# Which PSUM banks the five two-bank products of the second feed-forward matmul take

## The chip, the cores and the metric

The kernel runs on one core of a Trainium2 chip. The metric is device microseconds (us) of one execution, lower is better. One execution was also taken by the hardware profiler, and every row below is from it.

## The reference

A two-layer transformer block on 512 tokens of width 1024 in float32. Each layer is a mixer (convolution, pooling, gating and sparse attention) and a feed-forward half; only the latter matters here:

```python
for l in range(2):
    ...
    h = rms_norm(x, pre_ffn_norm[l])
    f = jnp.square(jax.nn.relu(jnp.einsum('bsd,df->bsf', h, ffn_w1[l])))   # 512x1024 @ 1024x4096
    x = x + rms_norm(jnp.einsum('bsf,fd->bsd', f, ffn_w2[l]), post_ffn_norm[l])  # 512x4096 @ 4096x1024
```

## The kernel before, in words

**Precision.** Every float32 operand is split into a high and a low part, `wh` and `wl` for weights (`split`: one ScalarE activation for the high part, one VectorE subtraction for the low one). `mm3` replaces one product by three matmuls (high by high, high by low, low by high).

**The feed-forward half.** `ffn` cuts the 4096 hidden columns into four parts. In parts 0, 1 and 2 both matmuls are done by a seven-product scheme (Strassen-like) on 2 by 2 blocks. `square4` makes the hidden values of half a part: its products A11, A12, S1, S2, S3, S4, A22 run as 128x256 matmuls into `pf` banks, and VectorE and ScalarE turn them into the forms `A11` to `S4` that the second matmul reads (a form's high half by ScalarE, its low half by VectorE). The second matmul's seven products are p1, p7, p2, p5, p6, p3 and q4, in this order, as 128x512 matmuls, 24 for each product: two token halves by two weight units by six. p1 and p7 keep banks of their own for all three parts (`po`). The other five ask `banks()` for two PSUM banks (`pm`), one for each half, and `add_up` adds each half to a sum in SBUF when it is done: ScalarE copies in part 0, VectorE additions (`acc<-pm,acc`, or `y<-pm,y` for p2 and q4) in parts 1 and 2. Part 3 is done in the ordinary way.

**PSUM.** Eight banks in four groups: `mm` three, `o` one, `s` two (p7's here), `x` two (p1's here). `square4`'s `pf` tiles also use `mm` and `o`. A bank is free for the next tile when its last reader is done.

**Weights.** `load` brings 512 KB units from HBM on SyncE's queue into six raw buffers `wr`. Some products want a sum of weight blocks: `more` adds a further block to a raw buffer by an accumulating DMA on GpSimd's queue (POOL). p5's two units get one each, p7's two get one and then, after they were split, another for p6 and another for q4. An accumulate into a buffer waits until the load, or the split, before it is done.

**What sets the order.** `_Rec` records all operations, and `order()` then writes the order of every engine by list scheduling: it has a cost for each operation, a delay for each pair of engines, and the number of buffers of each pool, and takes at each step the operation that can start first by these. So a change of a bank's group can move instructions on every engine, and whatever is late on the chip is waited for in that fixed order, since each engine works its list from front to back. All instructions show as line 442 (`issue`).

Of the kernel before, what the change touches and what calls it, by code (L numbers as in the profile page):

```python
# [19 lines left out]
P = 128  # L20
# [424 lines left out]
SUMS, CONV, POST, FORM, FORM2, FORM3, C11 = 300, -300, -1000, -1000, 0, 500, 500  # L445


TAGS = "mm", "o"
FIN = (1, 1), (1, 0)


class _Net:
# [907 lines left out]
    def ffn(self, l, norm):  # L1360


        (_, (F, _)), y = norm
        ssv = self.small.tile([P, NT, 2], F32, name=self.nm("ssv"), tag="ssv", bufs=2)
        accs = [y, self.big("acc", F32), self.big("acc", F32)]
        acc = {"q4": accs[0][:, 0:2], "p2": accs[0][:, 2:4], "p5": accs[1][:, 0:2], "p6": accs[1][:, 2:4],
               "p3": accs[2][:, 0:2]}

        own = {"p1": [self.pst([P, 512], "po", "x") for _ in range(2)],
               "p7": [self.pst([P, 512], "po", "s") for _ in range(2)]}  # L1370

        u0 = U_FF
        for part in range(NPART - 1):
            uw = u0 + PART
            form, raw = {}, {}

            def put(name, bh, v):
                if name not in form:
                    form[name] = self.big(name)
                o = slice(2 * bh, 2 * bh + 2)  # L1380
                hi = form[name][:, o, :256]
                self.act(hi, v)
                self.tt(form[name][:, o, 256:], v, hi.bitcast(F32), ALU.subtract)

            def emit0(bh, th, v):
                raw["A21" if th else "A11", bh] = v
                if not th:
                    put("A11", bh, v)
                if ("A11", bh) in raw and ("A21", bh) in raw:
                    s3 = self.scr("s3").rearrange("p (b q) -> p b q", b=2)  # L1390
                    self.tt(s3, raw["A11", bh], raw["A21", bh], ALU.subtract)
                    put("S3", bh, s3)

            def emit1(bh, th, v):
                raw["A22" if th else "A12", bh] = v
                if not th:
                    put("A12", bh, v)
                if ("A12", bh) in raw and ("A22", bh) in raw:
                    a11, a21, a12, a22 = (raw[n, bh] for n in ("A11", "A21", "A12", "A22"))
                    self.tt(a21, a22, a21, ALU.subtract)  # L1400
                    put("S1", bh, a21)
                    self.stt(a11, a21, -1.0, a11, ALU.mult, ALU.subtract)
                    put("S2", bh, a11)
                    self.stt(a12, a11, -1.0, a12, ALU.mult, ALU.subtract)
                    put("S4", bh, a12)
                    put("A22", bh, a22)

            def banks():
                return [self.pst([P, 512], "pm", TAGS[i]) for i in range(2)]

            def product(pss, units, a, first=True, final=True):

                for u in range(2):
                    wh, wl = units(u)
                    for t in range(2):
                        c = slice(P * t, P * t + P)
                        d = slice(256 + P * t, 256 + P * t + P)
                        for kk in range(2):
                            k = 2 * u + kk
                            o = slice(512 * kk, 512 * kk + 512)  # L1420
                            self.mm3(pss[t], a[:, k, c], a[:, k, d], wh[:, o], wl[:, o], first and k == 0,
                                     final and k == 3)

            def add_up(name, pss):
                for i in range(2):
                    v = acc[name][:, i]
                    if part == 0:
                        self.act(v, pss[i])
                    else:
                        self.tt(v, pss[i], v, ALU.add)  # L1430

            more = lambda x, i: self.nc.gpsimd.dma_start(x, self.a["wst"][l, i], accum_op=ALU.add)
            sq = [self.square4(l, u0 + 4 * i, F, e, y[:, i] if part == 0 else None)
                  for i, e in enumerate((emit0, emit1))]
            if part == 0:
                for _ in range(2):
                    for v in sq:
                        next(v)
            for _ in sq[0]:
                pass  # L1440

            raws = {}
            simple = lambda i: lambda j: self.split(self.load(l, uw + i + j))

            def weights(first, j, *steps):

                if (first, j) not in raws:
                    raws[first, j] = self.load(l, uw + first + j)
                x = raws[first, j]
                for i in steps:  # L1450
                    more(x, uw + i + j)
                return self.split(x)


            steps = {"p1": simple(0), "p2": simple(2), "p3": simple(6), "p5": lambda j: weights(0, j, 4),
                     "p7": lambda j: weights(4, j, 6), "p6": lambda j: weights(4, j, 0),
                     "q4": lambda j: weights(4, j, 2)}
            left = {"p1": "A11", "p7": "S3", "p2": "A12", "p5": "S1", "p6": "S2", "p3": "S4", "q4": "A22"}
            for name in ["p1", "", "p7", "p2", "p5", "p6", "p3", "q4"]:
                if not name:  # L1460
                    for _ in sq[1]:
                        pass
                elif name in own:

                    product(own[name], steps[name], form[left[name]], part == 0, part == NPART - 2)
                else:
                    ps = banks()
                    product(ps, steps[name], form[left[name]])
                    add_up(name, ps)
            u0 += 2 * PART  # L1470

        plus = lambda v, w: self.tt(v, w, v, ALU.add)
        f = [[self.big("f") for _ in range(2)] for _ in range(2)]

        def emit(i):
            def put(bh, th, v):
                o = slice(None), slice(2 * bh, 2 * bh + 2), slice(256 * th, 256 * th + 256)
                self.act(f[0][i][o], v)
                self.tt(f[1][i][o], v, f[0][i][o].bitcast(F32), ALU.subtract)
            return put  # L1480


        ys = {}
        self.nc.shift = SUMS
        for i in range(2):
            y11, y12, y21, U, w = (acc[n][:, i] for n in ("p2", "p3", "q4", "p6", "p5"))
            plus(U, own["p1"][i])
            plus(y11, own["p1"][i])
            plus(w, U)
            plus(y21, U)  # L1490
            plus(y12, w)
            plus(w, own["p7"][i])
            plus(y21, own["p7"][i])
            ys[i, 0], ys[i, 1], ys[2 + i, 0], ys[2 + i, 1] = y11, y12, y21, w
        self.nc.shift = 0
        for i in range(2):
            for _ in self.square4(l, u0 + 4 * i, F, emit(i)):
                pass
        srcs = [(f[0][k // 4][:, k % 4], f[1][k // 4][:, k % 4]) for k in range(PART)]
        g2, g0 = self.gains(*[(l, 3072), (l + 1, 0)][:1 + (l + 1 < L)])  # L1500
        uw = u0 + PART
        for t, ps in self.tgroup(lambda j: self.unit(l, uw + j), srcs, 2):
            v = ys[t, 0]
            plus(v, ps)
            self.square(v, ssv[:, t, 0:1])
            self.tt(v, v, g2[:, 0:512], ALU.mult)
        after = (g0, self.new_hT()) if l + 1 < L else None
        for t, ps in self.tgroup(lambda j: self.unit(l, uw + 4 + j), srcs, 4, own["p1"] + own["p7"]):
            v = ys[t, 1]
            self.nc.shift = POST  # L1510
            self.tt(v, ps, v, ALU.subtract)
            self.square(v, ssv[:, t, 1:2])
            self.nc.shift = 0
            self.tt(v, v, g2[:, 512:], ALU.mult)
            self.post(t, [ys[t, 0], v], ssv[:, t])
            if after:
                self.norm_tile(t, *after)
        return after
# [82 lines left out]
```

## Time and profile before

| | us |
|---|---|
| median of 3 runs | 1053.36 (1053.11, 1053.36, 1060.53) |
| profiled execution | 1053.45 |
| its span in the trace | 1051.7 |
| TensorE busy in the span | 1024.9 |
| VectorE busy | 824.8 |
| ScalarE busy | 611.0 |

PE is TensorE, DVE VectorE, ACT ScalarE, POOL GpSimd, SP SyncE. The ends of matmuls are modelled: a 128x512 matmul is shown with 0.39 us or more though the next one starts 0.23 us after it, so PE's busy time holds more than its pitch, and a wait costs a little more than the idle time that is shown. A group of rows such as `x2` stands for instructions in a row of one form. `[0.78 <-DVE acc]` says that the engine sat idle for 0.78 us before, and that a VectorE instruction writing `acc` ended it.

### The profile page before, as it was taken

The numbers are of one execution on the slowest core, as the hardware profiler recorded it, in microseconds if no ns is written. First come the engines' busy times: TensorE is split into PE (matmuls) and PEld (weight loads), VectorE is DVE, ScalarE is ACT, GpSimd is POOL, SyncE is SP. The second block draws the span as 40 slices with busy tenths as digits, with TensorE's granted clock in tenths as the row PEclk, the third lists the DMA queues.
The fourth block names the chain that finished last, engine by engine and source line by source line (L and its number), as shares of the span: only waits on it lengthen the run. The fifth ranks groups of instructions, "written<-read, shape, count | busy, mean of one in ns | idle before, by whom it ended". The sixth has DMA issues, their size and how long they took to land.

```text
span 1051.7 us, 17150 instructions
## 1 busy us (share of the span) xinstructions
PE 1024.9 (97%) x6706; PEld 891.7 (85%) x6706; DVE 824.8 (78%) x1250; ACT 611.0 (58%) x1057; POOL 137.6 (13%) x192
## 2 busy tenths in 40 slices
PE   7999999999999999999999999999999999999997
PEld 6998777898897898798899986779989978978985
DVE  7799976899478678976679998769985686798754
ACT  6437874676567366365444587658675655654731
POOL 3000011211121111110110000102211211211001
PEclk9999999999999999999999999999999999999999
DMA  8330244379989899986034110534998989989802
GB/s 296 115 122 21 61 124 115 73 186 232 227 217 229 222 245 216 215 248 215 22 95 138 60 56 26 120 101 98 223 224 212 235 207 235 243 189 245 232 4 80
DMA packets 47906, 168.89 MB, mean 161 GB/s; under 512 B 5713, under 2 KB 6609, under 8 KB 47570
## 3 DMA queue, kind: packets, MB, share of 16 engines
q0 software_dynamic: 16128, 58.73, 31.5%
q1 hardware_dynamic: 31698, 109.08, 30.2%
q8 instruction: 52, 0.85, 0.3%
q14 instruction: 28, 0.23, 0.1%
HBM read 165.69 MB, written 2.10 MB: 160 GB/s over the span
## 4 chain that ended last, share of the span: by engine, by line
PE 74%; DVE 11%; DMA 7%; issue 5%; ACT 3%; POOL 1%; POOLq 0%; DVEq 0%; SPq 0%; ACTq 0%
PE pf L442 24%; PE pm L442 22%; PE po L442 8%; PE pp L442 6%; DMA wr<-wst 6%; PE pc L442 3%; PE O L442 2%; PE s L442 2%; DVE wl L442 2%; PE ppt L442 2%; DVE cacc L442 2%; ACT wh L442 1%; PE pt L442 1%; POOL r L442 1%; PE ph L442 1%
## 5 line engine op out<-in xcount | busy, mean ns | idle before, releaser
L442 DVE TENSOR_TENSOR wl<-wr,wh 128x1024 fp32r<-128x1024 f32 (+1 forms) x256 | 305.0, 1205 | 95.1 <-ACT wh L442 93.8
L442 ACT ACTIVATE wh<-wr 128x1024 fp32r<-128x1024 f32 (+1 forms) x258 | 264.0, 1042 | 143.0 <-DMA wr<-wst 55.5
L442 PE MATMUL pf<-hF,wh 128*128 128x256 f32 x1728 | 300.8, 278 | 1.4 <-ACT wh L442 1.2
L442 PEld LDWEIGHTS pf<-hF,wh 128*128 128x128 f32 x1728 | 262.7, 188 | 6.3 <-ACT wh L442 2.2
L442 PE MATMUL pf<-hF,wl 128*128 128x256 f32 x864 | 239.0, 277 | 0.0
L442 POOL DMA_DIRECT2D wr<-wst x112 | 97.0, 900 | 511.6 <-DVE wl L442 255.2
L442 PEld LDWEIGHTS pf<-hF,wl 128*128 128x128 f32 x864 | 162.3, 188 | 0.8 <-DVE wl L442 0.2
L442 PE MATMUL pm<-wh,S 128*128 128x512 f32 x288 | 95.1, 400 | 6.5 <-DVE acc L442 4.1
L442 PE MATMUL pp<-wh,hT 128*128 128x256 f32 (+1 forms) x512 | 100.3, 287 | 0.0
L442 DVE SCALAR_TENSOR_TENSOR cacc<-rest,cwh,cacc 128x512 f32<-128x512 f32 x120 | 85.9, 742 | 0.4
L442 PE MATMUL pm<-wh,mixT 128*128 128x512 f32 x256 | 84.0, 401 | 1.2 <-DVE y L442 1.2
L442 PEld LDWEIGHTS pp<-wh,hT 128*128 128x128 f32 x512 | 80.6, 188 | 0.5
L442 PEld LDWEIGHTS pm<-wh,S 128*128 128x128 f32 x288 | 53.8, 188 | 25.3 <-DVE acc L442 6.7
L442 PE MATMUL pp<-wl,hT 128*128 128x256 f32 (+1 forms) x256 | 74.0, 289 | 0.0
L442 PE MATMUL pm<-wh,A 128*128 128x512 f32 x192 | 63.0, 395 | 0.0
L442 PE MATMUL pm<-wl,S 128*128 128x512 f32 x144 | 56.7, 396 | 3.3 <-DVE wl L442 3.3
L442 PEld LDWEIGHTS pm<-wh,mixT 128*128 128x128 f32 x256 | 47.8, 188 | 13.2 <-DVE y L442 2.0
L442 ACT ACTIVATE c<-c 128x512 f32<-128x512 f32 x64 | 37.8, 622 | 24.7 <-DVE c L442 24.4
L442 PE MATMUL pm<-wl,mixT 128*128 128x512 f32 x128 | 50.6, 395 | 0.0
L442 PEld LDWEIGHTS pp<-wl,hT 128*128 128x128 f32 x256 | 48.2, 188 | 0.3
L442 PE MATMUL pc<-hT,wh 128*128 128x256 f32 x256 | 47.4, 287 | 0.8 <-ACT hT L442 0.8
L442 POOL TENSOR_TENSOR r<-rs,mhalf 128x1 f32<-128x1 f32 x32 | 24.0, 750 | 158.2 <-DVE rs L442 158.2
(283 smaller groups left out, 1841.1 us busy)
## 6 DMA issues: line engine op xcount, KB each, us to landing
wr<-wst SPq DMA_DIRECT2D x182, 512.0 KB, 5.6
wr<-wst POOLq DMA_DIRECT2D x112, 512.0 KB, 7.1
gb<-rows SPq DMA_DIRECT2D x7, 512.0 KB, 5.9
wr<-wq SPq DMA_DIRECT2D x8, 268.0 KB, 2.8
xres<-x SPq DMA_DIRECT2D x4, 512.0 KB, 6.0
cw<-cw SPq DMA_DIRECT2D x2, 1024.0 KB, 7.2
out<-xres SPq DMA_DIRECT2D x3, 512.0 KB, 2.6
sgw<-sgw SPq DMA_DIRECT2D x2, 256.0 KB, 5.2
```

The costliest lines, as they stand in the source:

```text
L442: getattr(getattr(nc, e), method)(*[real(x) for x in args], **{k: real(x) for k, x in kw.items()})
```

## The change

`banks` gets the place `n` of the product in the list. A product at an odd place takes one `mm` bank and the `o` bank, one at an even place two `mm` banks. So p2 (3), p6 (5) and q4 (7) keep what they had, and p5 (4) and p3 (6) take two `mm` banks in place of one `mm` and the `o` bank. No operation is added or taken away; the order that `order()` writes differs on PE, ACT, DVE and POOL, and SP's is the same.

```diff
-TAGS = "mm", "o"
...
-            def banks():
-                return [self.pst([P, 512], "pm", TAGS[i]) for i in range(2)]
+            def banks(n):
+                return [self.pst([P, 512], "pm", "o" if i and n % 2 else "mm") for i in range(2)]
...
-            for name in ["p1", "", "p7", "p2", "p5", "p6", "p3", "q4"]:
+            for n, name in enumerate(["p1", "", "p7", "p2", "p5", "p6", "p3", "q4"]):
...
-                    ps = banks()
+                    ps = banks(n)
```

In the orders below a name carries the tile's number and then a number of its place, which differs between the two kernels; what counts is the first. `x2` is two in a row.

**PE where p5 begins, part 1 of layer 0.** `pm_579` and `pm_580` are p5's two halves, `pm_587` is p6's first half, `pm_593` p3's. Before:

```order
L442 MATMUL pm_572_3766<-wh_577_3676,A12_551_3624 128x512
L442 MATMUL pm_579_3800<-wh_582_3779,S1_559_3710 128x512
L442 MATMUL pm_587_3804<-wh_589_3759,S2_560_3719 128x512
L442 MATMUL pm_587_3804<-wl_590_3773,S2_560_3719 128x512
L442 MATMUL pm_587_3804<-wh_589_3759,S2_560_3719 128x512 x2
L442 MATMUL pm_587_3804<-wl_590_3773,S2_560_3719 128x512
L442 MATMUL pm_587_3804<-wh_589_3759,S2_560_3719 128x512
L442 MATMUL pm_587_3804<-wh_591_3787,S2_560_3719 128x512
L442 MATMUL pm_593_3820<-wh_596_3813,S4_561_3755 128x512
L442 MATMUL pm_580_3825<-wh_582_3779,S1_559_3710 128x512
L442 MATMUL pm_579_3800<-wl_583_3823,S1_559_3710 128x512
```

After:

```order
L442 MATMUL pm_572_3769<-wh_577_3678,A12_551_3624 128x512
L442 MATMUL pm_579_3801<-wh_582_3749,S1_559_3708 128x512
L442 MATMUL pm_579_3801<-wl_583_3761,S1_559_3708 128x512
L442 MATMUL pm_580_3807<-wh_582_3749,S1_559_3708 128x512
L442 MATMUL pm_580_3807<-wl_583_3761,S1_559_3708 128x512
L442 MATMUL pm_579_3801<-wh_582_3749,S1_559_3708 128x512 x2
L442 MATMUL pm_579_3801<-wl_583_3761,S1_559_3708 128x512
L442 MATMUL pm_579_3801<-wh_582_3749,S1_559_3708 128x512
L442 MATMUL pm_580_3807<-wh_582_3749,S1_559_3708 128x512 x2
L442 MATMUL pm_580_3807<-wl_583_3761,S1_559_3708 128x512
L442 MATMUL pm_580_3807<-wh_582_3749,S1_559_3708 128x512
L442 MATMUL pm_587_3827<-wh_589_3766,S2_560_3719 128x512
```

Both halves of p5's first unit now run ahead of p6, whose first half before came between p5's first matmul and the rest; p5's low part `wl_583` is wanted by the second matmul, not after ten of others.

**DVE at the same place.** `wl_583` is p5's first low part, `wl_592` p6's second, `s1_538` the end of `square4`'s last sum, `y_298` the sum of p2. Before, from the sum on:

```order
L442 TENSOR_TENSOR s1_502_3233<-s1_538_3524,s1_502_3233 128x512
L442 TENSOR_TENSOR wl_590_3773<-wr_565_3357,wh_589_3759 128x1024
...
L442 TENSOR_TENSOR S4_561_3755<-fr_550_3608,S4_561_3755 128x2x256
L442 TENSOR_TENSOR y_298_2077<-pm_572_3766,y_298_2077 128x512
L442 TENSOR_TENSOR wl_583_3823<-wr_581_3544,wh_582_3779 128x1024
L442 TENSOR_TENSOR wl_592_3827<-wr_568_3423,wh_591_3787 128x1024
```

After, from the same sum's first step on:

```order
L442 TENSOR_TENSOR s1_538_3518<-s1_538_3518,pf_542_3502 128x512
L442 TENSOR_TENSOR wl_583_3761<-wr_581_3550,wh_582_3749 128x1024
L442 TENSOR_TENSOR S4_561_3758<-c_558_3683,S4_561_3758 128x2x256
L442 SCALAR_TENSOR_TENSOR s1_538_3518<-s1_538_3518 128x512
L442 TENSOR_TENSOR wl_590_3781<-wr_565_3357,wh_589_3766 128x1024
L442 TENSOR_TENSOR s1_502_3241<-s1_538_3518,s1_502_3241 128x512
L442 TENSOR_TENSOR y_298_2077<-pm_571_3755,y_298_2077 128x512
...
L442 TENSOR_TENSOR y_298_2077<-pm_572_3769,y_298_2077 128x512
L442 TENSOR_TENSOR S4_561_3758<-fr_550_3609,S4_561_3758 128x2x256
L442 TENSOR_TENSOR wl_592_3842<-wr_568_3452,wh_591_3787 128x1024
L442 TENSOR_TENSOR wl_586_3849<-wr_584_3675,wh_585_3838 128x1024
```

`wl_583` has moved to the front of the chain of sums and forms. After it stand twelve operations of 128x512, the low part `wl_590`, and then `wl_592` and `wl_586`.

**POOL, the accumulates of part 1 of layer 0.** `wr_503` and `wr_539` hold the weights of the first and the second `square4`, `wr_581` and `wr_584` p5's units, `wr_565` and `wr_568` those that serve p7, p6 and q4. Before:

```order
L442 DMA wr_503_3071<-wst 128x1024 x2
L442 DMA wr_539_3251<-wst 128x1024
L442 DMA wr_535_3211<-wst 128x1024
L442 DMA wr_539_3251<-wst 128x1024
L442 DMA wr_565_3357<-wst 128x1024
L442 DMA wr_568_3423<-wst 128x1024
L442 DMA wr_539_3251<-wst 128x1024
L442 DMA wr_565_3357<-wst 128x1024
L442 DMA wr_568_3423<-wst 128x1024
L442 DMA wr_581_3544<-wst 128x1024
L442 DMA wr_565_3357<-wst 128x1024
L442 DMA wr_584_3683<-wst 128x1024
```

After:

```order
L442 DMA wr_503_3072<-wst 128x1024
L442 DMA wr_539_3236<-wst 128x1024
L442 DMA wr_503_3072<-wst 128x1024
L442 DMA wr_535_3193<-wst 128x1024
L442 DMA wr_539_3236<-wst 128x1024
L442 DMA wr_565_3357<-wst 128x1024
L442 DMA wr_568_3452<-wst 128x1024
L442 DMA wr_539_3236<-wst 128x1024
L442 DMA wr_565_3357<-wst 128x1024
L442 DMA wr_581_3550<-wst 128x1024
L442 DMA wr_568_3452<-wst 128x1024
L442 DMA wr_584_3675<-wst 128x1024
```

Two things moved in what the prediction uses: the last accumulate into `wr_503` (the first `square4`'s product A22) now goes behind the first one into `wr_539`, and p5's accumulate into `wr_581` goes ahead of p6's into `wr_568`.

**Part 2.** There twelve of p2's 24 matmuls now run ahead of A22, so that 15 matmuls of 128x512 stand between the end of A22 and p5's first one, where 27 stood before. (In part 1 it is 25 in both kernels: one of p7's and p2's 24.) On DVE the sum behind A22 is followed in part 2 by eleven more operations of 128x512 and p6's first low part `wl_699`, and then by p5's second low part `wl_695`; before, both of p5's low parts stood behind these forms. Layer 1 has the same moves as layer 0, with other numbers. Outside `ffn` nothing moves.

## Rows read from the trace of the kernel before

**Rows 1.** The page: span, busy times, and matmuls beside which nothing waits (busy, mean ns).

```profile
span 1051.7 us, 17150 instructions
...
PE 1024.9 (97%) x6706; PEld 891.7 (85%) x6706; DVE 824.8 (78%) x1250; ACT 611.0 (58%) x1057; POOL 137.6 (13%) x192
...
L442 PE MATMUL pm<-wl,mixT 128*128 128x512 f32 x128 | 50.6, 395 | 0.0
```

**Rows 2.** Stretches: length; PE, PEld, DVE, ACT, POOL busy; clock; DMA share; GB/s.

```profile
205.00:285.00 80.00, 79.90 (x521) 71.56 (x520) 65.58 (x85) 55.92 (x82) 14.66 (x17) 1.00 0.86 205
285.00:443.00 158.00, 152.98 (x983) 135.14 (x982) 124.23 (x152) 88.98 (x115) 27.63 (x32) 1.00 0.92 226
```

**Rows 3.** PE's waits, 205 to 530: us in total, times, longest.

```profile
PE pm L442 <- DVE acc L442: 2.1, 2, 1.4
PE pm L442 <- DVE wl L442: 1.7, 2, 1.0
PE pm L442 <- ACT wh L442: 0.5, 2, 0.3
...
PE pm L442 <- DVE S L442: 0.3, 1, 0.3
PE pm L442 <- DVE y L442: 0.3, 1, 0.3
```

**Rows 4.** PE's waits in layer 1, 715 to 1046; its other rows read alike.

```profile
PE pm L442 <- DVE acc L442: 1.9, 2, 1.2
...
PE pm L442 <- ACT wh L442: 0.6, 2, 0.3
```

**Rows 5.** The chain through 253 to 300: start, length, engine and matmuls.

```profile
254.52 24.90 PE pm L442 x108
...
282.44 16.23 PE pf L442 x143
```

**Rows 6.** Timeline in part 1, layer 0: start, length, instruction, idle before.

```profile
339.85 0.68 DVE L442 TENSOR_TENSOR y<-pm,y 128x512 f32<-128x512 f32 x1
340.45 2.35 DVE L442 TENSOR_TENSOR wl<-wr,wh 128x1024 fp32r<-128x1024 f32 x2
340.59 0.50 PE L442 MATMUL pm<-wh,S 128*128 128x512 f32 x1 [0.27 <-DVE y L442]
...
341.72 0.50 PE L442 MATMUL pm<-wl,S 128*128 128x512 f32 x1 [0.63 <-DVE wl L442]
```

**Rows 7.** The same view, ten us later.

```profile
350.74 0.69 DVE L442 TENSOR_TENSOR acc<-pm,acc 128x512 f32<-128x512 f32 x1 [0.46 <-PE pm L442]
...
351.49 0.50 PE L442 MATMUL pm<-wh,S 128*128 128x512 f32 x1 [0.78 <-DVE acc L442]
```

**Rows 8.** The same view of PE in part 2.

```profile
422.04 0.50 PE L442 MATMUL pm<-wl,S 128*128 128x512 f32 x1 [1.04 <-DVE wl L442]
...
435.42 0.50 PE L442 MATMUL pm<-wh,S 128*128 128x512 f32 x1 [1.35 <-DVE acc L442]
```

**Rows 9.** Part 1: the issue of p5's first accumulate, and the sum behind A22.

```profile
326.02 0.84 POOL L442 DMA_DIRECT2D wr<-wst  x1 [2.33 <-DMA wr<-wst]
...
331.36 0.69 DVE L442 TENSOR_TENSOR s<-s,pf 128x512 f32<-128x512 f32 x1 [0.59 <-PE pf L442]
```

**Rows 10.** That accumulate among the DMA issues: KB, us to landing.

```profile
wr<-wst POOLq DMA_DIRECT2D x1, 512.0 KB, 8.4
```

**Rows 11.** The two accumulates issued at 292.0 and 292.6: us to landing.

```profile
DMA to landing us min/median/max: 5.5/8.1/10.7
```

**Rows 12.** ACT's split of the unit that the second of these filled.

```profile
303.40 1.06 ACT L442 ACTIVATE wh<-wr 128x1024 fp32r<-128x1024 f32 x1 [0.99 <-DMA wr<-wst]
```

**Rows 13.** All accumulates of 285 to 443: landing; packets, MB, share of 16 engines.

```profile
DMA to landing us min/median/max: 5.4/7.4/10.9
...
q0 software_dynamic: 4588, 16.72, 58.4%
```

**Rows 14.** Part 2: VectorE's sum behind A22.

```profile
411.58 0.69 DVE L442 TENSOR_TENSOR s<-s,pf 128x512 f32<-128x512 f32 x1 [0.67 <-PE pf L442]
```

## The prediction

> **What bounds the kernel now.** I began with the page's head: TensorE is busy for 1024.9 of 1051.7 us, and no other engine is above 824.8 [rows 1]. What can be won by an order that computes the same is therefore PE's idle time, 27 us in all, and only the part of it that this change touches. Next I cut the feed-forward halves into stretches. In part 0 of layer 0 PE is busy for 79.90 of 80.00 us, so a bank can win nothing there; in parts 1 and 2 it is busy for 152.98 of 158.00 [rows 2]. The difference is `add_up`: part 0 copies out by ScalarE, parts 1 and 2 add by VectorE. The granted clock is 1.00 throughout, so it plays no part.
>
> The table of PE's waits says what ended the idle time. In layer 0 it names `acc` 2.1 us, `wl` 1.7, `wh` 0.5, `S` 0.3 and `y` 0.3 [rows 3], and in layer 1 `acc` 1.9, `wh` 0.6, and the other three as before [rows 4]. These are 4.9 and 4.8 us in eight waits each. A matmul's shown end hides a piece of each wait: matmuls follow each other at a pitch of 24.90/108 = 0.23 us (128x512) and 16.23/143 = 0.1135 us (128x256) [rows 5], but a 128x512 one is shown with 0.395 where nothing waits [rows 1]. So each wait costs 0.16 us more than is shown, 1.3 us per layer. **At stake are 4.9 + 4.8 + 2.6 = 12.3 us**, all behind the single `o` bank, as two places show:
>
> - At 340.59 PE waits 0.27 us for `y` [rows 6]: p2's second half sits in the `o` bank until VectorE's add of 339.85 is done, and only then can p5's second half begin. In the meantime the order has run pieces of p6 and p3 ahead, which want forms and weights sooner than needed, so PE also waits for `S`, `wh` and, 0.63 us at 341.72, `wl`.
> - At 351.49 PE waits 0.78 us for `acc` [rows 7]: p6's second half needs the `o` bank that VectorE's add of 350.74 has just freed from p5's. In part 2 this wait is 1.35 us, and the `wl` wait 1.04 [rows 8].
>
> So the direct waits for a bank are `acc` 4.0 + `y` 0.6 in six waits, 4.6 + 6 × 0.16 = **5.5 us**; the other ten, for forms and weights, cost 12.3 − 5.5 = **6.8 us**.
>
> **The change part by part.** Nothing is computed more or less, so the sum is made of waits removed and waits added.
>
> *Removed, −12.3.* p5 no longer takes `o`, so its two halves run in one stretch, and p6's second half finds `o` freed by p2 a whole product earlier (24 × 0.23 = 5.5 us, against one add of 0.69). p3 likewise leaves `o` to q4. The six bank waits go. The other ten go as far as the pieces run ahead were their cause; what replaces them is priced below.
>
> *Added (1): A22 of part 1's first half waits for its weights.* Two accumulates were issued at 292.0 and 292.6, and one landed after 5.5 us, the other after 10.7 [rows 11], at 303.3; ACT's split of the late one started at 303.40 when it landed, after 0.99 us idle [rows 12]. Before, A22's buffer was the first of the pair; now it is the second. PE gets there after the S4 product, whose `pf` run ends at 282.44 + 16.23 = 298.7, and twelve of p1's matmuls and 17 of the next half's A11: 298.6 + 12 × 0.23 + 17 × 0.1135 = 303.3 (a run's shown end is 0.1 past its pitch). Weights: 303.40 + 1.06 for the split, and 0.06 to hand over, as from the end of VectorE's add to PE's matmul at 351.49 [rows 7], make 304.5. Wait 1.2, for two layers **+2.4**. Below it is 0 (if the engines serve both so that either lands in time), above 1.2 + 2.9 per layer, if one more accumulate (priced below) comes first.
>
> *Added (2): p5's weights in part 1.* p5's low part is now wanted by its second matmul, and VectorE does it in front of its chain of sums and forms. Let its accumulate land at L. Then p5's first low part is done at L + 1.0 + 1.2 = L + 2.2 (1.06 [rows 12] and half of 2.35 [rows 6]). Behind it in VectorE's order stand twelve operations at a pitch of 0.60 (339.85 to 340.45 [rows 6]), one low part of 1.2, and p6's second low part, another 1.2: done at L + 2.2 + 9.6 = L + 11.8, and p5's second one at L + 13.0. PE reaches p5 25 matmuls after A22's end at 331.3 [rows 9], so at 337.1, and wants p6's second low part 27 matmuls later, at 343.3. So PE waits L + 11.9 − 343.3, and then 0.5 more for the last low part (1.2 less the three matmuls between): L − 330.9 in all. What is L? Before, the accumulate was issued at 326.02 when its load had landed, and took 8.4 us [rows 9, 10]: L = 334.4, a wait of 3.5 per layer. But then p6's accumulate was queued ahead of it, and now it is behind. One accumulate takes 58.4% of 158 us over 32 = 2.9 us of all 16 engines [rows 2, 13], so L = 334.4 − 2.9 = 331.5, and 5.5 us after the issue is about the shortest landing of the stretch [rows 13]. I take it, since the removal of what was served ahead has a row for its size: wait 0.6, two layers **+1.2**. The ends are 0 (issued a little earlier) and 6.0 per layer (10.9 us, the longest landing).
>
> *Added (3): the same in part 2.* There A22 is moved nearer to p5: 15 matmuls between them, not 27. PE's arrival at p5 doesn't change: 411.5 [rows 14] + 27 × 0.23 = 417.7; so A22 now ends at 417.7 − 15 × 0.23 = 414.2. Behind it VectorE has twelve operations of 0.60 and two low parts of 1.2, 9.6 us, before p5's second low part is there: 423.8 + 0.1. PE wants it 26 matmuls after p5's start, at 423.7. Wait 0.2, if p5's first low part is done before the sum; if it comes in between, 1.2 more, and a stop for ScalarE's split with it, 1.8. Between them I take 0.8, nearer to the lower one since p5's accumulate goes ahead of p6's here too: **+1.6** for two layers.
>
> *Added (4): other moves on PE* at the start of part 2's halves. The nearest rows are the short waits of 0.3 [rows 3]; I take one for each layer, **+0.6**, between none and three for each.
>
> SyncE's order is the same, so the loads cost nothing. In part 0 the copies are ScalarE's, with no wait to remove, and PE has 0.1 us idle to lose: 0.
>
> **Sum:** 1053.45 − 12.3 + 2.4 + 1.2 + 1.6 + 0.6 = **1047.0 us**. The profiled execution stands 0.1 above the median of the runs shown, which I neglect. The forecast's own range is 1043.5 (terms 1 and 4 at nothing, 3 at its lower end) to 1050.8 (the accumulate takes the median 7.4 us [rows 13], L = 333.4, wait 2.5 per layer).
>
> **The rivals.** *A: all waits go and none comes.* 1053.45 − 12.3 = 1041.2. For it: the same idle times recur in each part that adds by VectorE and in no other, which is what a missing bank looks like. Against it: term (1) rests on a landing that the trace shows. The Trainium skill has a rule for this side (Perfetto Trace Analysis, section "Optimization Strategy"): a gap that repeats on the engine that should be saturated can mean that PSUM has no room for the next tile. The trace agrees for the waits named `acc` and `y`, and not for those named `wl` and `wh`.
>
> *B, slower: the accumulate lands as late as before or later.* p5's low part now stands at the head of VectorE's list, so every us of lateness goes through the forms and low parts to PE. At 8.4 us the waits are 3.5 in part 1 and 1.8 in part 2 per layer: −12.3 + 2.4 + 7.0 + 3.6 + 0.6 = +1.3, 1054.8; at 10.9 us, 6.0 in part 1, 1059.8. It decides from the point at which the added waits reach 12.3: (12.3 − 2.4 − 3.6 − 0.6) / 2 = 2.85 per layer, L = 333.8, 7.7 us after the issue. For it: the DMA engines are at 0.92 in these stretches [rows 2], so there is little room for anything to land sooner. Against: what was ahead in the same queue is gone.
>
> *C: only the direct waits for a bank go.* VectorE's list is as long as before, 124.23 of 158.00 us busy in bursts, and PE's waits for forms and low parts stay in one shape or another in place of terms (2) and (3): 1053.45 − 5.5 + 2.4 + 0.6 = 1051.0.
>
> That the change does not do what it says is no rival: the order shows both halves of p5 in a row.
>
> **How the numbers follow.** Forecast 0.55; A 0.12; B 0.18; C 0.15. The range holds the forecast's own range and C, and B to its first price; it leaves out A and B's tail, about 0.2: 1043 to 1055. Within 1%, about what a measurement of this kernel can tell from no change, is 1042.8 to 1063.9: faster 0.12 (A), slower 0.02 (B's far tail), the same 0.86.
>
> **What would show it.** In the trace of the changed kernel PE's waits for `acc` and `y` in parts 1 and 2 should be gone; if one of 0.5 us or more stays, the removal is wrong. Step (1): a wait of some 1 us for `wh` in a `pf` matmul near 303, and the same in layer 1. Steps (2) and (3): short waits of `pm` for `wl`, 0.6 and 0.8 per part; if they are 2 us or more and the accumulate of p5 landed 7.7 us or more after its issue, it is B. PE's idle time in 285 to 443 should fall from 5.0 to some 2.5 us. I am wrong if a wait comes that I haven't priced, above all on ScalarE, where p5's split now stands ahead of two forms and p6's split: it stops there until the accumulate lands.

## The result and the profile after

The changed kernel takes 1042.74 us (median of four runs, 1041.60 to 1044.16) beside 1054.09 for the kernel before: 11.4 us less by the medians; the ratio is 0.9882, interval 0.9861 to 0.9903, which is 12.4 us of 1054.09. The prediction was 1047.0 with a range of 1043 to 1055, so the time lies 0.3 us below the range, near rival A (1041.2); one of the four runs lies inside it. The profiled execution took 1041.60, 11.85 us less than the one before.

The head of the page of the changed kernel, to hold against [rows 1]: PE's busy time is 3.5 us less and the span 11.8 us less, so it is idle time that went, and a little busy time that was only matmuls held up.

```profile
span 1039.9 us, 17135 instructions
...
PE 1021.4 (98%) x6706; PEld 894.6 (86%) x6706; DVE 823.5 (79%) x1250; ACT 610.1 (59%) x1057; POOL 137.6 (13%) x192
```

PE's waits in the changed kernel, first 205 to 520 us, then 704 to 1040 (layer 1), each row total, times and longest. Against [rows 3, 4] every wait named `acc`, `y`, `wh` and `wl` of a `pm` matmul is gone; what is left before p5 is a form, `S`, and one wait of a `pf` matmul.

```profile
PE pm L442 <- ACT S L442: 1.3, 2, 0.9
PE pf L442 <- DVE wl L442: 0.9, 1, 0.9
...
PE pm L442 <- ACT S L442: 0.5, 1, 0.5
```

The stretch 285 to 443 of layer 0, as in [rows 2], of the changed kernel: 2.2 us idle in place of 5.0.

```profile
285.00:443.00 158.00, 155.81 (x1012) 140.03 (x1011) 125.08 (x154) 90.63 (x119) 27.11 (x32) 1.00 0.91 225
```

For the account I cut each trace at the same instructions. These are windows from the end of p2 to the end of q4 (p5, p6, p3 and q4, 96 matmuls), for parts 1 and 2 of both layers, counting `pm` only: length, then PE's busy time. First the kernel before:

```profile
336.88:362.84 25.96, 23.74 (x97) 17.37 (x95) 5.55 (x9) 0.00 (x0) 1.00 0.91 223
417.56:443.68 26.12, 23.32 (x97) 17.41 (x95) 5.37 (x8) 0.00 (x0) 1.00 0.91 218
854.90:880.85 25.95, 23.73 (x97) 17.37 (x95) 5.54 (x9) 0.00 (x0) 1.00 0.93 223
935.57:961.50 25.93, 23.29 (x97) 17.41 (x95) 5.38 (x8) 0.00 (x0) 1.00 0.82 204
```

and the changed kernel, same columns:

```profile
336.91:360.24 23.33, 22.48 (x97) 17.87 (x96) 5.88 (x9) 0.00 (x0) 1.00 0.86 222
415.33:438.21 22.88, 22.47 (x97) 17.87 (x96) 5.13 (x8) 0.00 (x0) 1.00 0.80 191
848.14:870.42 22.28, 22.28 (x97) 17.83 (x96) 5.21 (x8) 0.00 (x0) 1.00 0.84 217
926.06:949.02 22.96, 22.49 (x97) 17.87 (x96) 5.23 (x8) 0.00 (x0) 1.00 0.80 190
```

The sums are 103.96 and 91.45 us. These four windows hold 12.5 us, all of the gain and 0.7 more. The third window of the changed kernel shows no wait, so 22.28 us is what the work takes: before, 14.8 us were lost in the four windows, after, 2.3.

### The profile page after: what moved, and what is told of

The parts are those of the page before. It is cut to its first block, busy times and chain, and to the rows that moved or that the text cites. A ratio compares the mean times of both kernels' runs of the same rounds, so it can differ in the third digit from the quotient of the medians.

```text
span 1039.9 us, 17135 instructions
## 1 busy us (share of the span) xinstructions
PE 1021.4 (98%) x6706; PEld 894.6 (86%) x6706; DVE 823.5 (79%) x1250; ACT 610.1 (59%) x1057; POOL 137.6 (13%) x192
## 4 chain that ended last, share of the span: by engine, by line
PE 80%; DVE 10%; DMA 3%; ACT 3%; issue 2%; POOL 1%; POOLq 0%; DVEq 0%; SPq 0%; ACTq 0%
PE pf L442 28%; PE pm L442 23%; PE po L442 9%; PE pp L442 6%; PE pc L442 3%; DMA wr<-wst 3%; PE O L442 2%; DVE wl L442 2%; PE s L442 2%; PE ppt L442 2%; DVE cacc L442 2%; DVE h L442 1%; PE pt L442 1%; ACT wh L442 1%; POOL r L442 1%
## 5 line engine op out<-in xcount | busy, mean ns | idle before, releaser
L442 PE MATMUL pm<-wh,S 128*128 128x512 f32 x288 | 90.6, 395 | 1.7 <-ACT S L442 1.7
```

The lines of the kernel that those rows point to most:

```text
L442: getattr(getattr(nc, e), method)(*[real(x) for x in args], **{k: real(x) for k, x in kw.items()})
```

## The experiments

All ratios are to the kernel before, run beside on the same chip. The time behind each is the median.

**Which of the products matters: p5 alone.** The banks in the diffs of the next six runs stand in the changed kernel's line.

```diff
-                return [self.pst([P, 512], "pm", "o" if i and n % 2 else "mm") for i in range(2)]
+                return [self.pst([P, 512], "pm", "o" if i and n != 4 else "mm") for i in range(2)]
```

> Only p5 takes two mm banks; p3 keeps one mm and the o bank. The accumulates' order is that of the changed kernel. Theory 1 (the gain is the o bank: each product that takes it straight after another one that has it waits for a VectorE addition): p3's second half now waits for p6's second half, about 0.8 shown + 0.16 in four parts, so some 3.8 us of the 12 come back: about 1046.5. Rival (what the changed kernel won comes from the new order of the accumulates on POOL and from the splits): nothing comes back, 1042.7.

Measured: 0.9877 (0.9862 to 0.9892), 1041.8. Nothing came back, so theory 1 in this form (every hand-over of the `o` bank costs) is wrong: p3 and q4 still take the bank after p6, and the trace has one `acc` wait of 0.4 us, q4's. The rival, by which the gain lies in the other engines' orders, isn't excluded by this run, as their orders are those of the changed kernel.

**p3 alone** (`n != 6`).

> Only p3 takes two mm banks; p5 keeps one mm and the o bank, between p2 and p6 which have it too. Theory 1: p5's second half still waits for p2's and p6's for p5's, so the acc and y waits stay and most of the loss with them: 1050 to 1054. Rival (each of the two edits is worth half): about 1048.

Measured: 0.9907 (0.9884 to 0.9929), 1044.61. Most of the gain is there although p5 keeps the `o` bank between p2 and p6. Theory 1 falls again, and "half each" too.

**No product on the o bank.**

```diff
-                return [self.pst([P, 512], "pm", "o" if i and n % 2 else "mm") for i in range(2)]
+                return [self.pst([P, 512], "pm", "mm") for i in range(2)]
```

> All five products take two of the three mm banks and none the o bank. Theory 1 in its wider form (a product waits when one of its banks was the one before's): with three banks each product shares one with the one before, so waits named acc come back in parts 1 and 2, as many as before or more: 1050 to 1056. Rival (only the single o bank is slow, since it cannot rotate): 1042 to 1044.

Measured: 0.9923 (0.9903 to 0.9942), 1047.2, between the two. Waits for a bank are there again in the feed-forward halves (`y` 2.0 us and `acc` by ScalarE 1.4, over both layers), but they cost less than the ones before.

**Four banks of one group.**

```diff
-    PSUM_TAGS = {"mm": 3, "o": 1, "s": 2, "x": 2}
+    PSUM_TAGS = {"mm": 4, "s": 2, "x": 2}
...
     def pst(self, shape, name, tag="x"):
+        tag = "mm" if tag == "o" else tag
```

> The o bank becomes a fourth mm bank, in the whole kernel, so any two products in a row have banks of their own without the alternation. Theory 1: no wait for a bank is left, as in the changed kernel; 1040 to 1044. Rival (the fixed places of the o bank in the mixer and in square4 are worth something by themselves): slower than the changed kernel, 1046 or more, with new waits outside the second product.

Measured: 1.0216 (1.0199 to 1.0233), 1077.35. The rival decides the time, and by far. Its windows by stage (length, PE busy; the clock is the third number from the end) show where: the feed-forward half of layer 0, second row, is as free of waits as in the changed kernel, as theory 1 has it, and in the mixer, first row, PE is busy for ten us less than in the changed kernel's same stretch, third row.

```profile
0.00:205.00 205.00, 188.41 (x1228) 154.67 (x1229) 153.24 (x307) 111.87 (x249) 18.91 (x45) 0.97 0.36 113
205.00:445.00 240.00, 238.99 (x1551) 214.83 (x1550) 191.08 (x242) 153.26 (x221) 43.64 (x52) 1.00 0.85 205
...
0.00:205.00 205.00, 198.66 (x1329) 165.79 (x1329) 168.07 (x333) 123.70 (x276) 22.36 (x52) 1.00 0.38 116
```

**p2 alone** (`n != 3`). With p3 a surprise, I asked whether any product will do. This kernel is the cleanest of the study: VectorE, ScalarE, POOL and SP keep the order of the kernel before to the last instruction.

> Only p2 takes two mm banks; p5, p6, p3 and q4 keep one mm and the o bank. The order of VectorE, ScalarE, POOL and SP is then that of the kernel before to the last instruction, and PE's differs in 54 rows: p5's second half comes a little earlier. Theory 2 (PE loses where several products have opened their first halves in mm banks and their second halves queue one behind the other for the o bank; p6 and p3 still do so behind p5): the y waits go, 0.6 + 0.3, the acc waits and the wl waits stay: 1051 to 1054. Rival (any one product less on the o bank is enough, as one of p5 and p3 was): 1043 to 1046.

Measured: 1.0023 (1.0007 to 1.0040), 1056.53: nothing gained. The waits of `pm` in layer 0, 205 to 530 us, against [rows 3]: of `acc` one of two is left (in layer 1 both are, 1.3 us), and `y` has grown from 0.3 to 1.1: by the kernel's order the matmul that waits is the first of p3, and it wants p2's second `mm` bank.

```profile
PE pm L442 <- DVE wl L442: 1.6, 2, 1.0
PE pm L442 <- DVE y L442: 1.1, 1, 1.1
PE pm L442 <- DVE acc L442: 0.8, 1, 0.8
```

**q4 alone** (`n != 7`).

> Only q4, the last of the five, takes two mm banks; p2, p5, p6 and p3 keep the o bank. Theory 2: three halves are still opened ahead and queue for the o bank (p5, p6, p3), and nothing but q4's own hand-over goes: 1049 to 1053. Rival (q4's 24 matmuls can be run ahead in mm banks while the others wait, as p3's could): 1043 to 1046.

Measured: 0.9929 (0.9901 to 0.9957), 1046.89. Theory 2 expected 1049 or more, and the rival is right: p5, p6 and p3 do queue for the `o` bank here, and PE hardly waits. How, is seen at one hand-over. In the kernel before, the last matmul into p5's half begins at 350.31, and p6's first into the same bank at 351.49 [rows 7], 1.18 us later, with nothing between:

```profile
350.31 0.40 PE L442 MATMUL pm<-wh,S 128*128 128x512 f32 x1
...
351.83 0.39 PE L442 MATMUL pm<-wl,S 128*128 128x512 f32 x1
```

With q4 alone changed, p5's half ends at about 346.2, VectorE's add runs from 347.00 to 347.68, and p6's half begins with the second of the two matmuls of 347.79; the eight matmuls from 346.19 on (1.84 us) are p3's first half, which the list of the kernel before had used up ahead of p5's last matmuls:

```profile
346.42 0.62 PE L442 MATMUL pm<-wh,S 128*128 128x512 f32 x2
...
347.00 0.68 DVE L442 TENSOR_TENSOR acc<-pm,acc 128x512 f32<-128x512 f32 x1
...
347.79 0.62 PE L442 MATMUL pm<-wh,S 128*128 128x512 f32 x2
```

So a hand-over is 1.18 us from matmul to matmul, five pitches of 0.23, and costs only what the list has not put between, provided that VectorE comes at once. Call this theory 3; it was read from the traces afterwards, and no run was made to test it. By the kernels' orders no matmul stands between p5's half and p6's in part 1 of the kernel before and of the p2 kernel, eight do in the q4 and p3 kernels, and with p5 in `mm` banks the two no longer share one.

Theory 3 is not the whole, as the kernel before shows at its longest wait, 1.35 us at 435.42 in part 2 [rows 8]. There p3's half waits for p6's add, and by the order nine matmuls stand between the two users, eight of p3's first half and the one of q4 in the second line below. That is more than a hand-over asks for. But VectorE's list has a low part ahead of the add, and stands still for it, since ScalarE can split those weights only at 432.44, when they have landed:

```profile
432.44 2.01 ACT L442 ACTIVATE wh<-wr 128x1024 fp32r<-128x1024 f32 x2 [3.30 <-DMA wr<-wst]
...
433.54 1.23 DVE L442 TENSOR_TENSOR wl<-wr,wh 128x1024 fp32r<-128x1024 f32 x1 [1.56 <-ACT wh L442]
...
433.68 0.39 PE L442 MATMUL pm<-wh,A 128*128 128x512 f32 x1
...
434.68 0.68 DVE L442 TENSOR_TENSOR acc<-pm,acc 128x512 f32<-128x512 f32 x1
```

The changed kernel's list has the same add ahead of the same low part. VectorE stands just as long for the split, and PE doesn't notice:

```profile
427.99 0.68 DVE L442 TENSOR_TENSOR acc<-pm,acc 128x512 f32<-128x512 f32 x1
...
433.81 1.23 DVE L442 TENSOR_TENSOR wl<-wr,wh 128x1024 fp32r<-128x1024 f32 x1 [1.57 <-ACT wh L442]
```

Layer 1 has the same two places. So of the `acc` waits of the kernel before some 1.6 us (0.8 in part 1 of each layer) are hand-overs with nothing between, and some 2.5 (1.35 and 1.2, in part 2) are weights that landed late, passed on by the place of an add in VectorE's list. The `y` wait of 0.27 at 340.59 is of the second kind too, without the landing: by the order nine matmuls stand between, but VectorE, busy without a break since 331.36 [rows 9], gets to p2's add only at 339.85 [rows 6].

**The price of a late landing.** Nothing but the place of p5's first accumulate, on POOL's queue in parts 1 and 2, is changed in the finished list.

```diff
     seq = rec.order()
+    for i, j in rec.swap:
+        seq.remove(i)
+        seq.insert(seq.index(j) + 1, i)
```

(`i` is the accumulate into p5's first buffer, `j` p6's second one.)

> The changed kernel with one thing moved by hand in the finished order: in parts 1 and 2 p5's first accumulate goes behind p6's second one on POOL's queue, as it did before; no other instruction moves. Theory of the prediction's term 2 (ScalarE and VectorE stop for p5's split, and PE's wait grows with the landing): landing some 3 us later, PE's wait before p5 from 0.9 to 4 or 5 in part 1 of both layers, and some of it in part 2: 1049 to 1052. Rival (the order has slack that takes it up): 1043 to 1044.

Measured: 1.0142 (1.0111 to 1.0172), 1069.18, 26 us above the changed kernel and 15 above the one before. The direction is the theory's, the size three times what I expected, for two reasons. The landing came more than 3 us later, and PE waited in all four parts: ScalarE's split, which waits for it, begins at 337.33 where the changed kernel's begins at 331.95 (below), and PE's four waits are of 4.3 to 5.4 us:

```profile
PE pm L443 <- ACT S L443: 19.8, 4, 5.4
...
337.33 1.06 ACT L443 ACTIVATE wh<-wr 128x1024 fp32r<-128x1024 f32 x1 [7.76 <-DMA wr<-wst]
...
343.30 0.80 PE L443 MATMUL pm<-wh,S 128*128 128x512 f32 x1 [5.26 <-ACT S L443]
```

And after the wait TensorE runs slower. The same kernel's windows (PE's busy time and matmuls second, its granted clock third from the end):

```profile
338.00:343.30 5.30, 0.04 (x1) 0.00 (x1) 4.88 (x7) 3.48 (x6) 0.86 (x1) 0.82 0.56 164
343.30:346.00 2.70, 2.70 (x6) 2.15 (x7) 2.70 (x5) 2.56 (x4) 0.00 (x0) 0.50 0.79 94
346.00:348.00 2.00, 2.00 (x6) 1.58 (x5) 2.00 (x5) 1.58 (x2) 0.00 (x0) 0.50 0.69 135
348.00:350.00 2.00, 2.00 (x9) 1.60 (x9) 1.35 (x2) 1.06 (x1) 0.23 (x1) 0.94 0.03 8
350.00:352.00 2.00, 2.00 (x10) 1.63 (x10) 2.00 (x2) 0.56 (x1) 0.64 (x1) 1.00 0.51 45
```

After 5.26 us without a matmul the clock is 0.50, its lower level of 1.2 GHz, until about 348.4, and twelve matmuls take some 0.43 us each in place of 0.23: 2.4 us more. The other three waits are followed by the lower clock too. 19.8 − 1.7 idle and 4 × 2 or so for the clock make the 26. The Trainium skill tells of this (TensorE: Matmul & The Clock Gate, section "Part 1: The HAM clock gate"): TensorE's clock depends on how busy it has lately been. The trace agrees, 0.50 against 1.00.

**Without p5's accumulates.**

```diff
-            steps = {"p1": simple(0), "p2": simple(2), "p3": simple(6), "p5": lambda j: weights(0, j, 4),
+            steps = {"p1": simple(0), "p2": simple(2), "p3": simple(6), "p5": lambda j: weights(0, j),
```

> The changed kernel without p5's accumulates (p5 multiplies by one weight block in place of a sum of two, so the output is another; 12 of 112 accumulates less, and the order is written anew). Theory: the waits before p5 named S go, 1.8 + 0.5, and nothing else, as the DMA engines aren't what PE waits for elsewhere: 1040 to 1041. Rival (transfers limit parts 1 and 2 more widely): below 1039.

Measured: 0.9842 (0.9815 to 0.9870), 1037.37: nearer to the rival, though the interval reaches up to the theory's 1040 to 1041. By the ratios it is 4 us below the changed kernel, by the medians 5, about twice what the `S` waits hold, and PE is busy without a break through parts 1 and 2 of layer 0:

```profile
285.00:443.00 158.00, 158.00 (x1046) 144.11 (x1046) 128.31 (x156) 93.10 (x119) 24.99 (x29) 1.00 0.88 215
```

So what is left to gain there hangs on the accumulates; as the whole list is written anew, this run doesn't say by which of them.

**The place of A22's accumulate.** Moved back by hand, in part 1 of both layers.

```diff
     seq = rec.order()
+    f = {(l, u, i): k for l, u, _, i, k in rec.acc}
+    for (l, u, i), k in f.items():
+        j = f.get((l, u + 4, 3))
+        if i == 1 and j and u == 37 and seq.index(k) > seq.index(j):
+            seq.remove(k)
+            seq.insert(seq.index(j), k)
```

> The changed kernel with one thing moved by hand in part 1 of both layers: the last accumulate of the first square4's A22 goes ahead of the second square4's first one again, as before the change. The prediction's term 1 (A22 waits for it 1.2 us per layer) would gain 2.4: 1040.3. Theory now (its weights are ready 0.9 us before PE wants them, so the place of the accumulate costs nothing): 1042.7, no wait named wh at A22 in either kernel.

Measured: 0.9886 (0.9866 to 0.9907), 1042.58. Within the interval, nothing. But this is no clean test of the prediction's term 1, and the expected absence of a wait at A22 did not come true: in the profiled execution PE waits for A22's own weights, 0.5 us in layer 0 and 2.4 in layer 1, where the changed kernel does not. Only POOL's list was moved back. On ScalarE the split for the second `square4` still stands ahead of A22's; it now waits for the accumulate that lands last, until 812.00 in layer 1, and A22's split comes behind it:

```profile
812.00 1.06 ACT L444 ACTIVATE wh<-wr 128x1024 fp32r<-128x1024 f32 x1 [5.46 <-DMA wr<-wst]
...
815.04 1.04 ACT L444 ACTIVATE wh<-wr 128x1024 fp32r<-128x1024 f32 x1
...
816.13 0.50 PE L444 MATMUL pf<-hF,wh 128*128 128x256 f32 x2 [2.37 <-ACT wh L444]
```

**The last waits before p5, moved by hand.** In the first of these runs one step of the sum in part 2 ran ahead of the addition that feeds it, so that sum is another; the second has this mended.

```diff
     seq = rec.order()
+    for i, j in rec.move:
+        if seq.index(i) > seq.index(j):
+            seq.remove(i)
+            seq.insert(seq.index(j), i)
```

> The changed kernel with three instructions moved by hand in parts 1 and 2: on VectorE the two steps of the sum behind A22 go ahead of p5's first low part, on ScalarE the high half of S1 that follows from them goes ahead of p6's second split. Theory (what PE waits for before p5 is this form, held up by the splits of weights that land late): the waits named S, 1.8 idle and 0.5 more hidden, go: 1040.4. Rival (p5's low part, done later now, is waited for in their place): 1042 to 1044.

Measured: 0.9869 (0.9855 to 0.9882), 1040.75, with 0.5 us of `S` waits left.

```diff
+        if rec.ops[i][0] == "vector":
+            at = max([seq.index(j)] + [seq.index(d) + 1 for d, _ in rec.ops[i][4]])
+            if at < seq.index(i):
+                seq.remove(i)
+                seq.insert(at, i)
+        if rec.ops[i][0] == "scalar" and seq.index(i) < seq.index(j):
+            seq.remove(i)
+            seq.insert(seq.index(j) + 1, i)
```

> The run before once more with every result kept: in parts 1 and 2 the sum behind A22 is finished before p5's first low part where its input allows that (in part 2 it comes right behind it, before p6's low part), and p6's second split on ScalarE goes behind the high half of S1. Theory: the waits named S go, 1.8 idle and 0.5 more hidden: 1040.4, ratio to the kernel before 0.986. Rival (p5's or p6's weights are then waited for instead): 1042 to 1044, ratio 0.988 or more.

Measured: 0.9874 (0.9854 to 0.9894), 1042.33, no better than the changed kernel. PE's wait for ScalarE's half of `S` is gone and one for VectorE's half has come:

```profile
PE pm L443 <- DVE S L443: 2.2, 4, 0.8
```

The rival holds in another shape: not p5's weights but the low half of the same form is late next.

> The same moves by hand with only p5 on two mm banks. Theory: as the run beside it, since p3's banks are worth nothing once p5 has two: within 1 us of it, 1040 to 1041. Rival (with the S waits gone p3's wait for the o bank comes to the fore): 1042 or more.

(The same two pieces of code with `n != 4` in `banks`.) Measured: 0.9880 (0.9862 to 0.9897), 1042.83. The interval doesn't separate it from its neighbour or from the changed kernel; two `acc` waits, of 0.7 and 0.8, are in its trace. No run that computes the whole beats the changed kernel beyond its interval, p5 alone being its equal.

## Why the prediction was wrong

The waits that the forecast said would go went, and a wait for p5's weights came, as it said. The sum failed in two steps, both in the same direction: it removed less than the chip did, 12.3 for 14.8, and it added 2.4 for a wait that did not come. They make 4.9 of the 5.3 us between −6.5 and −11.8.

The lower end of the forecast's own range is also added up wrongly. Terms 1 and 4 at nothing and term 3 at its lower end of 0.2 per layer give 1053.45 − 12.3 + 1.2 + 0.4 = 1042.8, not 1043.5, and the stated range, which was drawn to hold that figure, begins at 1043. The 0.3 us by which the time misses it are less than this slip and less than the spread of the four runs; the middle of the forecast is what was wrong.

**Removed: 14.8, not 12.3.** This term was too small by 2.5. The waits counted were the right ones, and all went, those for `wl`, `wh` and `S` too, as forecast. The mistake in size is the 0.16 us that I put behind each wait for what its shown end hides. At 351.49 the wait shows 0.78 us [rows 7], but the matmuls around it begin at 350.31 and 351.83: 1.52 us for two pitches of 0.23, a loss of 1.06, so 0.28 behind the wait: the one after it is late too. Sixteen waits by 0.28 and 9.7 shown make 14.2; the last 0.6 would be in gaps too short for the list. The figure of 0.28 is from one wait, but the four windows of the kernel before bear it out: 9.9 us of them are shown idle, and 14.8 are lost. One reading was wrong as well: "all behind the single `o` bank". In part 2 the direct wait is not p6's for p5's bank but p3's for p6's, and it hung on a late landing in front of VectorE's add, as shown above for the q4 run. In the p5 run p3 still takes the bank after p6, with seven matmuls between, and this wait is gone in both layers; its one `acc` wait, 0.4 us, is of q4. So the new list is enough to take it away, without a second `mm` bank for p3.

**Added (1), A22's weights: 0, not 2.4.** This is the step that failed outright: a wait was put on the path that did not arise. The pair of accumulates landed after 5.6 and 9.6 us (the group below), not 5.5 and 10.7 [rows 11], and it was issued 1.1 us earlier, at 290.9 and 291.5, since the load ahead of it landed earlier. So the split began at 301.21, not at 303.4 [rows 12], and PE came for it at 303.21. I took one landing of one execution as fixed where the chain that leads to it had 2 us of play, and PE's wait of 1.2 was smaller than that. The margin is thin: in layer 0 the weights were ready 0.9 us before PE came, in layer 1, where the split began at 813.06 and PE came at 814.3, only 0.1. So the mechanism of term 1 is not refuted; it did not bind in this execution, and with the accumulates in the old order under the new ScalarE list it did (0.5 and 2.4 us, above).

```profile
DMA to landing us min/median/max: 5.6/7.6/9.6
...
301.21 1.06 ACT L442 ACTIVATE wh<-wr 128x1024 fp32r<-128x1024 f32 x1 [0.17 <-DMA wr<-wst]
...
813.06 1.06 ACT L442 ACTIVATE wh<-wr 128x1024 fp32r<-128x1024 f32 x1 [0.89 <-DMA wr<-wst]
```

**Added (2) and (3), p5's weights: 2.3, forecast 2.8.** The size is right. p5's accumulate landed 6.5 us after its issue at 325.38, at 331.9; the forecast said 331.5, and its formula, L − 330.9, gives 1.0 for the part 1 of layer 0, where PE waited 0.85 and a little more. Not right is who waits. I took p6's second low part for the consumer that comes too late; PE stops already at p5's first matmul, 337.92, for a form that the chain of sums ends in. The timeline of that place in the changed kernel:

```profile
331.95 1.06 ACT L442 ACTIVATE wh<-wr 128x1024 fp32r<-128x1024 f32 x1 [3.35 <-DMA wr<-wst]
...
333.04 1.22 DVE L442 TENSOR_TENSOR wl<-wr,wh 128x1024 fp32r<-128x1024 f32 x1 [0.97 <-ACT wh L442]
...
336.29 1.06 ACT L442 ACTIVATE wh<-wr 128x1024 fp32r<-128x1024 f32 x1 [1.81 <-DMA wr<-wst]
336.52 0.68 DVE L442 TENSOR_TENSOR s<-s,s 128x512 f32<-128x512 f32 x1
...
337.25 0.61 ACT L442 ACTIVATE S<-s 128x512 fp32r<-128x512 f32 x1
...
337.92 0.50 PE L442 MATMUL pm<-wh,S 128*128 128x512 f32 x1 [0.85 <-ACT S L442]
```

VectorE stands 0.97 us before p5's low part, until the weights have landed and been split, and the sum `s` comes out at 337.2; ScalarE stands before p6's second split until 336.29; `S` can't be before 337.8. The last paragraph of the prediction named this stop of ScalarE as what could go wrong. In layer 1 part 1 there is no wait at all, which is the spread between two layers of one execution.

**Added (4), other moves: with the rest 0.7, forecast 0.6.** All that lies outside the four windows comes to 12.5 − 11.8 = +0.7. It is made of pieces of either sign: 0.35 us less before the feed-forward half begins, 0.45 and 1.1 less in the two parts 0, 0.7 less up to p5 in part 1 of layer 1 (where the kernel before has a `pf` wait for `wh` of 0.8 us at A22 that I hadn't counted), and a new `pf` wait for `wl` of 0.9. The remaining 2.4 us more are put down to stretches in which the matmuls of square4 follow more slowly, of which one, of 0.7, is shown in the last section. That the term came out right is luck: it was put at two waits of 0.3.

Put together, −14.8 + 0 + 2.3 + 0.7 = −11.8 from the kernel before's profiled execution.

**The rivals.** A was the nearest time, though not for its reason: waits did come, 2.3 us, and more than it reckoned went. B's mechanism is real and was underpriced: the run with the late accumulate lost 26 us, since its accumulate landed later still (the split begins at 337.33, where B's longest landing gives 336.9) and each wait was followed by the lower clock, which no row of the kernel before shows. Its condition did not hold here: with p6's accumulate behind it, p5's landed 2 us sooner after the issue than before, as the forecast argued. C is refuted: the waits for forms and low parts went, and 2.3 us came in their place, not 6.8.

What the forecast didn't see at all is that the banks matter through the list that is written for them. Every assignment with one product moved, except p2's, removes more than half of the loss, and what decides is whether matmuls of other work stand between two users of the single bank and whether VectorE's list lets the add run in time. It did not ask the list either: `order()` leaves the end of its own plan in `rec.end`, and needs no chip for it. In its own costs this estimate is 7.5 us lower for the changed kernel than for the one before, the same 7.5 for p5 alone, 6.1 for q4 alone, nothing for p2 alone, and 22.5 higher for the four banks of one group; by the ratios the runs are 12.4, 13.0 and 7.5 lower, and 2.4 and 22.8 higher.

**What stays open:** how much of the gain is due to the hand-overs, and how much to the new orders of VectorE, ScalarE and POOL that came with every one of the good assignments. The traces tell the `acc` waits apart (1.6 us of hand-overs, and 2.5 of a list held up, which the p5 run shows gone without new banks for p3), not the ten waits for forms and weights. The p2 run, where those orders stayed, doesn't decide it, since there p5, p6 and p3 still hand the bank on as before; a run with the new lists and the old banks wasn't tried on the chip.

## What to carry to other kernels

Where one buffer is handed from product to product, measure the hand-over from matmul to matmul (here 1.18 us), turn it into instructions of the waiting engine (five), and look whether the order has that many between two users, and whether the engine that empties the buffer has something in front that can be late (here a wait of 1.35 us with nine matmuls between). Where a scheduler writes the order, ask it for its own estimate first. Count a wait from the starts of the instructions around it, not from the idle time shown (0.28 us more here). A price that rests on one transfer's landing is worth no more than the play of the transfers ahead of it, some 2 us here, and the wait of 5.3 us here cost half as much again through the clock.

## What the runs showed of the hardware

TensorE's fall to 0.50 of its clock after 5.3 us without a matmul, and some 5 us until it was back at 1.00, is shown above.

The pitch of matmuls isn't constant at a granted clock of 1.00. In the same stretch of the same work, without a wait, the kernel before ran 142 matmuls and the changed kernel 136:

```profile
283.00:299.00 16.00, 16.00 (x142) 15.92 (x141) 10.37 (x12) 9.61 (x14) 3.06 (x4) 1.00 0.80 204
...
283.00:299.00 16.00, 16.00 (x136) 15.91 (x135) 10.10 (x11) 10.55 (x13) 2.60 (x3) 1.00 0.84 185
```

(the first row is of the kernel before, the second of the changed one). That is 0.113 and 0.118 us, 0.7 us in this stretch. The kernel before has the slower pitch too, 36.75 us for 312 matmuls of 128x256 from 443.84 on:

```profile
443.84 36.75 PE pf L442 x312
```

So it comes and goes within one execution; its cause is open.
